# A decoder layer on one core: the opening with eight gate blocks per row block and half of x read turned, and four convolution blocks held behind points of VectorE's order

## The chip, the cores and the metric

The program runs on one core of one Trainium2 chip. The metric is the device time of one launch in microseconds (us). The profile comes from one further execution of the same program.

Names of the engines: TensorE (PE) multiplies matrices, with weight loads (PEld) beside them; VectorE (DVE), ScalarE (ACT) and GpSimd (POOL) work on tiles; SyncE (SP) only issues DMAs here. Each engine works through its own instructions in order, and waits on semaphores of the others.

## The reference

One layer of a hybrid decoder, D = 1024, 512 tokens, all in float32:

```
mod = silu(c) @ ada_w + ada_b;  sh1, sc1, g1, sh2, sc2, g2 = split(mod, 6)
u = rms_norm(x, mix_pre_g) * (1 + sc1) + sh1
qk_raw, v, o_pre, gates, glu = split(u @ w_in)
q, k = split(silu(causal_dwconv(qk_raw, 4 taps)))
h = mlstm_chunkwise(q, k, v, gates)          # 4 heads of 256, chunks of 128
h = rms_norm(h) * sigmoid(o_pre)
a, gt = split(glu)
y = silu(layer_norm(causal_dwconv(a * sigmoid(gt), 31 taps)))
mix = concat(h, y) @ w_out;  x = x + g1 * rms_norm(mix)
u = rms_norm(x, ffn_pre_g) * (1 + sc2) + sh2
a, gt = split(causal_dwconv(u @ ffn_up, 3 taps))
x = x + g2 * rms_norm((silu(gt) * a) @ ffn_down)
```

The change concerns `u`, the `glu` columns, the 31-tap convolution, and through the order of VectorE the heads.

## The kernel before

**Layout.** Channels lie on partitions, tokens along the free axis. D makes 8 row blocks of 128 channels (`KT`), the tokens 4 tiles of 128 (`NT`). x arrives with tokens on partitions and has to be turned.

**Products.** Each operand is split into a high part rounded to the fast matmul type and a low part, the rest; a product is three matmuls, high·high, high·low, low·high, summed in PSUM (`mm3`, L188 to L190). ScalarE rounds the high part of a weight, GpSimd subtracts for the low part (`w_split`, L170, L171).

**Order.** TensorE and SyncE run in the order in which the program is written. The order on VectorE, ScalarE and GpSimd is chosen at build time by a list scheduler with priorities (`tc.cur_priority += LATER` puts work behind), except in a stretch under `in_order()`, which keeps the written order. `tc.add_manual_dep(..., NoSync ...)` makes one instruction stand behind another on its engine without a semaphore.

**Opening (L225 to L340, in order).** For each token tile VectorE and ScalarE sum x², VectorE makes `xs`, GpSimd its power −1/2, VectorE scales the two halves of x (`x_scale`, L237), and TensorE turns 128x128 blocks (`turn_x`, L232), 32 in all; ScalarE copies them out of PSUM (`x_out`). Then for each row block k:

- SyncE loads `adaT[k]` (1 MB, 128 x 2048, pool `raws` of two buffers, `first_load`) one row block ahead, and `w_glu0[k]` (six gate blocks, 128 x 768, pool `adas` of two buffers, L306).
- VectorE sums the two halves of `adaT[k]` against silu(c), which lies broadcast in PSUM (`cps`; `junk`, L319); two small operations make scale and shift (`gsk`, L322, L323).
- ScalarE makes u's high part `uh` (L328) and u itself (L330); GpSimd makes the low part `ul` (L331; VectorE for k = 0) and the weights' low parts.
- TensorE adds the row block to six PSUM banks, 6 x 3 matmuls of 128x512 (L338; for k < 2 pass by pass over the banks, afterwards bank by bank with `mm3`).

The six banks are gate blocks 0 to 2, each with a half `a` and a half `gt`. Blocks 3 to 7 follow with whole projections (ten banks, weights loaded 1 MB each). `glu_gate` (L352, L354) makes the convolution's input `gt`.

**Convolution.** Each of 8 channel blocks has 31 taps: ScalarE does one, 25 run on VectorE over a PSUM bank `cv` (L661), 5 as a `side` sum on ScalarE and GpSimd (L655, L657); `ydl` (L671) then adds to the moments. The loop stands behind the heads' code at lower priority (`LATER`), so the scheduler puts taps where VectorE would be free. The two `cv` banks come from `cvpool`, which takes the place of `cspool` (the PSUM of `cps`) once that is closed.

**Heads.** Per head six projections (`head_proj`; q and k pass a 4-tap convolution, `conv4`, L414, last tap `d = 3`), `v`, the decay `Md` (L535) and `E` (L540, L542) from `Mb` (L533), scores `s` (L455) that VectorE multiplies into `E` (L456), output `o` (L466), its norm `hn` (L482), turned by TensorE (`hT`, L488), times the gate `so` (L490), and split (`hh` L493, `hl` L494). `s`, `o` and `hT` share two PSUM banks (`atbank`): a bank is free when its reader is through.

**Modulation.** `ada_block(i)` (L153 to L155) loads half of an `adaT` block from ScalarE's queue into the two `adas` buffers, and VectorE sums it against `cb`, silu(c) in SBUF. Blocks 16 to 23 stand behind the last convolution tap. Mixing and ConvFFN follow; the change doesn't touch them.

Of the kernel before, what the change touches and what calls it, by code (L numbers as in the profile page):

```python
# [10 lines left out]
F32 = mybir.dt.float32  # L11
# [6 lines left out]
P = 128  # L18
D = 1024
# [33 lines left out]
def decoder_layer(ctx, tc, w_glu0, x, c, adaT, vecs, w_glu, w_qko, w_v0, w_v, w_out, w_up, w_down, out):  # L53
# [175 lines left out]
    nc.sync.dma_start(vec[:, :FIRST], vecs[:, :FIRST])  # L229
# [4 lines left out]
    xT_ps = [mmbank(f"xT{j}") if j % 6 < 4 else atbank(f"xT{j}") for j in range(KT)]  # L234
    def x_scale(tt, xs):
        for hf in range(2):
            V.tensor_scalar(out=xn[tt][hf], in0=xn[tt][hf], scalar1=xs[:, 1:], scalar2=None, op0=ALU.mult)  # L237
            for i in range(NT if hf == 0 else 2):
                turn_x(NT * hf + i, tt)
# [3 lines left out]
    xss = []  # L243
    xjunks = [slot(f"xjunk{hf}") for hf in range(2)]
    for tt in range(NT):
        xsq = small.tile([P, 2], F32, tag="adap", name=f"xsq{tt}")
        for hf in range(2):
            xjunk = xjunks[hf]
            if hf:
                V.scalar_tensor_tensor(out=xjunk, in0=xn[tt][hf], scalar=1.0, in1=xn[tt][hf], op0=ALU.mult, op1=ALU.mult, accum_out=xsq[:, hf:])  # L250
            else:
                S.activation(xjunk, xn[tt][hf], AF.Square, accum_out=xsq[:, :1])
        if tt:
            x_scale(tt - 1, xss[tt - 1])
        if tt == 1:
            S.activation(cb, cps, AF.Silu)
        if tt == NT - 1:
            S.activation(cps, cps, AF.Silu)
        xs = small.tile([P, 2], F32, tag="gsk", name=f"xs{tt}")
        V.tensor_scalar(out=xs[:, :1], in0=xsq[:, :1], scalar1=xsq[:, 1:], scalar2=D * EPS, op0=ALU.add, op1=ALU.add)  # L260
        G.tensor_tensor(out=xs[:, 1:], in0=xs[:, :1], in1=mhalf[:, :1], op=ALU.pow)
        xss.append(xs)
    x_scale(NT - 1, xss[-1])
# [7 lines left out]
    for j in range(6, KT):  # L271
        for tt in range(NT):
            turn_x(j, tt)
# [21 lines left out]
    G0 = 6  # L295
# [6 lines left out]
    banks0 = [mmbank(f"glu{i}") if i < 4 else atbank(f"glu{i}") for i in range(G0)]  # L302
    for k in range(KT):
        wk = []
        r = adas.tile([P, D], F32, tag="ada", name=f"wglu0_{k}")
        nc.sync.dma_start(r[:, : G0 * P], w_glu0[k])  # L306
        if k == 0:
            for j in range(3):
                x_out(j, S)
        for a, n in ((0, T), (T, (G0 - 4) * P)):  # L310
            wk.append(w_split(r[:, a : a + n], f"wglu0_{k}_{a}"))
# [4 lines left out]
        part = small.tile([P, 2], F32, tag="adap", name=f"adap{k}")  # L316
        for i in range(2):
            junk = small.tile([P, D], BF16, tag="junk", bufs=1, name=f"junk{k}_{i}")
            V.scalar_tensor_tensor(out=junk, in0=first[k][:, i * D : (i + 1) * D], scalar=1.0, in1=cps, op0=ALU.mult, op1=ALU.mult,  # L319
                                   accum_out=part[:, i : i + 1])  # L320
        gsk = small.tile([P, 2], F32, tag="gsk", name=f"gsk{k}")
        V.tensor_scalar(out=gsk[:, :1], in0=part[:, :1], scalar1=bp1[:, k : k + 1], scalar2=g32[:, k : k + 1], op0=ALU.add, op1=ALU.mult)  # L322
        V.tensor_scalar(out=gsk[:, 1:], in0=part[:, 1:], scalar1=vcol("ada_b", 2 * k + 1), scalar2=None, op0=ALU.add)  # L323
        if k == 0:
            x_out(3, S)
            V.tensor_scalar(out=xr[0], in0=xr[0], scalar1=gsk[:, :1], scalar2=gsk[:, 1:], op0=ALU.mult, op1=ALU.add)
        hi, lo = u[k]
        S.activation(hi, xT_ps[0] if k == 0 else xr[k], AF.Identity, scale=gsk[:, :1], bias=gsk[:, 1:])  # L328
        if k:
            S.activation(xr[k], xr[k], AF.Identity, scale=gsk[:, :1], bias=gsk[:, 1:])  # L330
        (G if k else V).tensor_tensor(out=lo, in0=xr[k], in1=hi.bitcast(F32), op=ALU.subtract)  # L331
        if k == 0:
            for j in (6, 7, 4, 5):
                x_out(j, S)
        if k < 2:
            for a, b in ((0, 0), (1, 0), (0, 1)):
                for i, ps in enumerate(banks0):
                    PE.matmul(ps, blk(wk, i)[a], u[k][b], start=k == 0 and a == b, stop=False)  # L338
# [6 lines left out]
    cspool.__exit__(None, None, None)  # L345
    cvpool.append(ctx.enter_context(tc.tile_pool(name="cvpool", bufs=2, space=PSUM)))
# [61 lines left out]
    def conv4(ps, i, name):  # L408
# [4 lines left out]
        for d in range(1, 4):  # L413
            V.scalar_tensor_tensor(out=t[:, d:], in0=ps[:, : T - d], scalar=w(3 - d), in1=t[:, d:], op0=ALU.mult, op1=ALU.add)  # L414
# [7 lines left out]
    heads = {}  # L422

# [6 lines left out]
    def head_proj(h, i):  # L430
# [113 lines left out]
    for i in range(3):  # L544
        head_proj(0, i)
# [708 lines left out]
```

## Time and profile before

| what | us |
|---|---|
| three runs | 781.28, 781.31, 781.71 |
| median | 781.31 |
| profiled execution | 782.39 |
| its span (first to last instruction) | 780.6 |
| TensorE busy | 761.7 |
| VectorE busy | 591.3 |
| ScalarE busy | 407.6 |
| GpSimd busy | 383.9 |

Starts in the trace count from the start of the span. The profiled execution lies 1.08 over the median, and its span leaves out 1.8 around it. In a row of the timeline stand start, duration, engine, line, operation, out<-in, form, count, and in brackets how long the engine was idle before it and who ended that. Matmuls overlap: their pitch is less than their duration.

### The profile page before, as it was taken

The page shows a single profiled execution, that of the slowest core. Times are in us where ns is not written, and L with a number is a line of the kernel's source. Part 1 is how long each engine was busy: PE and PEld are TensorE (multiplying, and loading weights), DVE is VectorE, ACT ScalarE, POOL GpSimd, SP SyncE. Part 2 cuts the span into 40 slices and gives each one's busy share as a digit, 9 for nine tenths or more (in the row PEclk, how much of TensorE's full clock was granted, in tenths as well). Part 3 has the DMA queues.
Part 4 walks back from the last instruction along what each step waited for, and adds up shares of the span by engine and source line. Part 5 has one row for each costly group of instructions (what it writes and reads, how often), then busy time and mean ns, then how long its engine had stood idle before and what let it go on. Part 6 is the DMA issues. An engine that isn't in the chain of part 4 may idle for free.

```text
span 780.6 us, 10572 instructions
## 1 busy us (share of the span) xinstructions
PE 761.7 (98%) x3683; PEld 635.0 (81%) x3683; DVE 591.3 (76%) x938; ACT 407.6 (52%) x766; POOL 383.9 (49%) x313
## 2 busy tenths in 40 slices
PE   7899999999999999999999999999999999999996
PEld 4678898878888888888878998888888888888884
DVE  7659999999998533555868799665556677699997
ACT  6576428668655554482244445444444444456762
POOL 3689759779778534334661446544454440000001
PEclk9999999999999999999999999999999999999998
DMA  8973313303117432424952763332333321777862
GB/s 297 325 293 126 107 58 108 135 29 109 55 57 248 154 103 86 143 105 144 391 196 103 242 230 136 129 108 93 124 115 128 116 101 61 260 273 235 299 241 108
DMA packets 35977, 124.28 MB, mean 159 GB/s; under 512 B 4146, under 2 KB 5586, under 8 KB 29908
## 3 DMA queue, kind: packets, MB, share of 16 engines
q1 hardware_dynamic: 24084, 95.15, 34.8%
q10 hardware_dynamic: 11840, 28.46, 10.2%
q8 instruction: 29, 0.48, 0.2%
q14 instruction: 24, 0.20, 0.1%
HBM read 112.17 MB, written 11.42 MB: 158 GB/s over the span
## 4 chain that ended last, share of the span: by engine, by line
PE 80%; DVE 10%; DMA 4%; issue 3%; POOL 1%; ACT 1%; ACTq 0%; POOLq 0%; DVEq 0%; SPq 0%
PE up L189 10%; PE up L188 10%; PE up L190 10%; DVE cv L661 5%; PE qko L188 4%; PE qko L189 4%; PE qko L190 4%; PE p L190 4%; PE p L189 4%; PE p L188 4%; PE glu L189 3%; PE glu L190 3%; PE glu L188 3%; DMA spare<-in_adaT 2%; PE o L466 2%
## 5 line engine op out<-in xcount | busy, mean ns | idle before, releaser
L661 DVE SCALAR_TENSOR_TENSOR cv<-gt,cvw,cv 128x506 f32<-128x506 f32 (+24 forms) x200 | 134.2, 728 | 0.4
L617 POOL TENSOR_TENSOR ro2r<-ro2t,mhalf 128x1 f32<-128x1 f32 x1 | 0.5, 538 | 120.7 <-DVE ro2t L615 120.7
L171 POOL TENSOR_TENSOR wup_1024l<-wup,wup_1024h 128x512 fp32r<-128x512 f32 x20 | 27.8, 1388 | 31.6 <-ACT wup_1024h L170 22.2
L171 POOL TENSOR_TENSOR wup_0l<-wup,wup_0h 128x512 fp32r<-128x512 f32 x20 | 27.8, 1388 | 29.4 <-ACT wup_0h L170 29.4
L657 POOL TENSOR_TENSOR cs<-cs,cs 128x510 f32<-128x510 f32 (+3 forms) x32 | 42.0, 1312 | 0.2
L171 POOL TENSOR_TENSOR wup_1536l<-wup,wup_1536h 128x512 fp32r<-128x512 f32 x20 | 28.4, 1422 | 27.2 <-ACT wup_1536h L170 27.2
L189 PE MATMUL up<-u2l,wup_0h 128*128 128x512 f32 (+1 forms) x100 | 36.5, 365 | 0.2 <-DVE u2l L830 0.2
L188 PE MATMUL up<-u2h,wup_0h 128*128 128x512 f32 (+1 forms) x100 | 36.5, 365 | 0.0
L188 PE MATMUL up<-u2h,wup_1024h 128*128 128x512 f32 (+1 forms) x100 | 36.4, 364 | 0.0
L190 PE MATMUL up<-u2h,wup_0l 128*128 128x512 f32 (+1 forms) x100 | 36.4, 364 | 0.0
L188 PE MATMUL up<-u2h,wup_512h 128*128 128x512 f32 (+1 forms) x100 | 36.4, 364 | 0.0
L189 PE MATMUL up<-u2l,wup_512h 128*128 128x512 f32 (+1 forms) x100 | 36.4, 364 | 0.0
L190 PE MATMUL up<-u2h,wup_512l 128*128 128x512 f32 (+1 forms) x100 | 36.4, 364 | 0.0
L188 PE MATMUL up<-u2h,wup_1536h 128*128 128x512 f32 (+1 forms) x100 | 36.4, 364 | 0.0
L189 PE MATMUL up<-u2l,wup_1536h 128*128 128x512 f32 (+1 forms) x100 | 36.4, 364 | 0.0
L190 PE MATMUL up<-u2h,wup_1536l 128*128 128x512 f32 (+1 forms) x100 | 36.4, 364 | 0.0
L190 PE MATMUL up<-u2h,wup_1024l 128*128 128x512 f32 (+1 forms) x100 | 36.4, 364 | 0.0
L189 PE MATMUL up<-u2l,wup_1024h 128*128 128x512 f32 (+1 forms) x100 | 36.3, 363 | 0.0
L155 DVE SCALAR_TENSOR_TENSOR junk<-ada,cb 128x1024 bf16<-128x1024 f32 x20 | 31.0, 1551 | 7.0 <-DMA ada<-in_adaT 6.7
L171 POOL TENSOR_TENSOR wup_512l<-wup,wup_512h 128x512 fp32r<-128x512 f32 x20 | 27.2, 1358 | 14.6 <-ACT wup_512h L170 14.6
L655 ACT ACTIVATE cs<-gt,cvw 128x511 f32<-128x511 f32 (+4 forms) x40 | 27.2, 712 | 5.0 <-POOL cs L657 4.1
L171 POOL TENSOR_TENSOR wqko_1024l<-wqko,wqko_1024h 128x512 fp32r<-128x512 f32 x12 | 16.6, 1380 | 21.9 <-PE v L189 12.3
(1061 smaller groups left out, 2680.6 us busy)
## 6 DMA issues: line engine op xcount, KB each, us to landing
wup<-in_w_up SPq DMA_DIRECT2D x22, 1024.0 KB, 8.3
wqko<-in_w_qko SPq DMA_DIRECT2D x12, 1024.0 KB, 5.0
ada<-in_adaT ACTq DMA_DIRECT2D x20, 512.0 KB, 5.9
ada<-in_adaT SPq DMA_DIRECT2D x16, 512.0 KB, 5.9
wo<-in_w_out SPq DMA_DIRECT2D x8, 1024.0 KB, 9.2
spare<-in_adaT ACTq DMA_DIRECT2D x12, 512.0 KB, 7.3
wglu<-in_w_glu SPq DMA_DIRECT2D x5, 1024.0 KB, 7.7
wd<-in_w_down SPq DMA_DIRECT2D x6, 768.0 KB
```

What stands on the lines that cost most here:

```text
L155: t = V.scalar_tensor_tensor(out=junk, in0=r, scalar=1.0, in1=cb, op0=ALU.mult, op1=ALU.mult, accum_out=mod[:, i : i + 1])
L171: (eng or G).tensor_tensor(out=lo[:, :n], in0=src, in1=hi[:, :n].bitcast(F32), op=ALU.subtract)
L188: PE.matmul(ps, a[0], b[0], start=start, stop=False)
L189: PE.matmul(ps, a[0], b[1], start=False, stop=False)
L190: PE.matmul(ps, a[1], b[0], start=False, stop=stop)
L466: PE.matmul(o[:, : DH + 2], E[h][cc][:, a : a + P], vs[h][cc], start=cc == 0, stop=cc == tt)
L617: G.tensor_tensor(out=r, in0=t, in1=mhalf[:, :1], op=ALU.pow)
L655: S.activation(t[:, d:], cvx[j][:, : T - d], AF.Copy, scale=w(CK - 1 - d))
L657: G.tensor_tensor(out=side[:, d:], in0=side[:, d:], in1=t[:, d:], op=ALU.add)
L661: last_tap = V.scalar_tensor_tensor(out=cp[:, d:], in0=cvx[j][:, : T - d], scalar=w(CK - 1 - d), in1=cp[:, d:], op0=ALU.mult, op1=ALU.add)
```

## The change

**Opening.** It takes eight gate blocks (`G0 = 8`, `w_glu0[k]` 128 x 1024): gate blocks 0 to 3; banks 6 and 7 are the two of `cvpool`, which opens earlier. Blocks 4 to 7 follow with eight projections. Only row blocks 0 to 3 of x are turned on TensorE, by a matmul with a diagonal tile `dg` (the identity times the token's factor, on VectorE, 128x128), which turns and scales at once; the same diagonal with `ones` gives the factors along the free axis (`rb`). Row blocks 4 to 7 come turned from memory (`xT`, 0.26 MB each, issued by SyncE in k = 1 to 4) and are scaled by VectorE (L348 of the new kernel). The sums run one row block ahead (`ada_sum(k + 1)`, around `ul`) and read `cb` in SBUF; all low parts are made on VectorE.

**Convolution.** The loop's body becomes `cv_block(j, behind)`. Blocks 0 to 3 are as before; the first tap of block 4 stands behind the last conv4 tap of head 0, of blocks 5, 6 and 7 behind those of projections (1, 0), (1, 3) and (2, 1).

```diff
-    def turn_x(j, tt):
-        PE.transpose(xT_ps[j][:, tt * P : (tt + 1) * P], xn[tt][j // NT][:, j % NT * P : (j % NT + 1) * P], ident)
...
-    def x_scale(tt, xs):
-        for hf in range(2):
-            V.tensor_scalar(out=xn[tt][hf], in0=xn[tt][hf], scalar1=xs[:, 1:], scalar2=None, op0=ALU.mult)
...
+    def x_turn(tt, xs):
+        dg = slot(f"dg{tt}")[:, :P]
+        V.tensor_scalar(out=dg, in0=ident, scalar1=xs[:, 1:], scalar2=None, op0=ALU.mult)
+        for j in range(TURNED):
+            PE.matmul(xT_ps[j][:, tt * P : (tt + 1) * P], xn[tt][j // NT][:, j % NT * P : (j % NT + 1) * P], dg, start=True, stop=True)
+        PE.matmul(rb_ps[:, tt * P : (tt + 1) * P], ones, dg, start=True, stop=True)
...
+    def ada_sum(k, i):
...
+        V.scalar_tensor_tensor(out=junk, in0=first[k][:, i * D : (i + 1) * D], scalar=1.0, in1=cb, op0=ALU.mult, op1=ALU.mult,
+                               accum_out=part[k][:, i : i + 1])
...
-    G0 = 6
+    G0 = 8
...
         if k == 1:
             nc.sync.dma_start(vec[:, FIRST:], vecs[:, FIRST:])
+        if 1 <= k <= TURNED:
+            j = TURNED + k - 1
+            nc.sync.dma_start(xr[j], xT[j - TURNED])
...
+        if k >= TURNED:
+            V.scalar_tensor_tensor(out=xr[k], in0=xr[k], scalar=gs, in1=rb, op0=ALU.mult, op1=ALU.mult)
+        for b in range(2):
+            wk[b] = w_split(r[:, b * T : (b + 1) * T], f"wglu0_{k}_{b}", eng=V)
...
+        if k + 1 < KT:
+            ada_sum(k + 1, 0)
+        if k < TURNED:
+            V.tensor_tensor(out=lo, in0=xr[k], in1=hi.bitcast(F32), op=ALU.subtract)
+        else:
+            V.scalar_tensor_tensor(out=lo, in0=xr[k], scalar=sh, in1=hi.bitcast(F32), op0=ALU.add, op1=ALU.subtract)
+        if k + 1 < KT:
+            ada_sum(k + 1, 1)
+        if k < 4:
+            passes(wk, k, range(G0))
         else:
...
+    CV_BEHIND = {(1, 0): 5, (1, 3): 6, (2, 1): 7}
...
+        if (h, i) in CV_BEHIND:
+            cv_block(CV_BEHIND[h, i], last_conv4[0])
...
+    head0_tap = last_conv4[0]
...
+            if behind is not None:
+                tc.add_manual_dep(last_tap[0].ins, behind.ins.name, mybir.DependencyInfo(mybir.DependencyClass.NoSync, mybir.DependencyReason.DATA),
+                                  reason="order on VectorE")
+                behind = None
...
+    for j in range(5):
+        cv_block(j, head0_tap if j == 4 else None)
```

VectorE in the opening, from the shift of one row block to that of the next but one; before:

```order
L323 TENSOR_SCALAR gsk_433<-adap_428,vec 128x1
L319 SCALAR_TENSOR_TENSOR junk_0_471,adap_470<-ada_425,cps 128x1024
L319 SCALAR_TENSOR_TENSOR junk_1_473,adap_470<-ada_425,cps 128x1024
L322 TENSOR_SCALAR gsk_475<-adap_470,bp_210,g_212 128x1
L323 TENSOR_SCALAR gsk_475<-adap_470,vec 128x1
```

and now, at row block 4 (`xr_221` its x, `rb_s` the factors, `wglu_4` its weights, `adap` the sums):

```order
L331 TENSOR_SCALAR gsk_440<-adap_404,bp_213,g_215 128x1
L332 TENSOR_SCALAR gsk_440<-adap_404,vec 128x1
L348 SCALAR_TENSOR_TENSOR xr_221<-xr_221,gsk_440,rb_s 128x512
L171 TENSOR_TENSOR wglu_4_0l<-wglu_4_434,wglu_4_0h 128x512
L171 TENSOR_TENSOR wglu_4_1l<-wglu_4_434,wglu_4_1h 128x512
L271 SCALAR_TENSOR_TENSOR junk_0_454,adap_453<-ada_436,cb 128x1024
L361 SCALAR_TENSOR_TENSOR ul<-xr_221,gsk_440,uh 128x512
L271 SCALAR_TENSOR_TENSOR junk_1_457,adap_453<-ada_436,cb 128x1024
L331 TENSOR_SCALAR gsk_488<-adap_453,bp_213,g_215 128x1
```

VectorE's four operations per row block have become eight, and the sums stand one row block ahead of their scale and shift.

VectorE ahead of head 0's `hn` (`cv_1699`, `cv_1748` and, in the new kernel, `cv_1702`, `cv_1877` are two blocks' sums of taps; the tap's number is 512 less the width); before, rows 303 to 309:

```order
L661 SCALAR_TENSOR_TENSOR cv_1699<-gt_874,cvw,cv_1699 128x491
L661 SCALAR_TENSOR_TENSOR cv_1748<-gt_945,cvw,cv_1748 128x499
L661 SCALAR_TENSOR_TENSOR cv_1699<-gt_874,cvw,cv_1699 128x490
L661 SCALAR_TENSOR_TENSOR cv_1748<-gt_945,cvw,cv_1748 128x498
L661 SCALAR_TENSOR_TENSOR cv_1699<-gt_874,cvw,cv_1699 128x489
L482 TENSOR_SCALAR hn_0_1962<-hn_0_1962,fac_2052 128x256 x2
L482 TENSOR_SCALAR hn_1_1963<-hn_1_1963,fac_2052 128x256 x2
```

and now, rows 302 to 308:

```order
L694 SCALAR_TENSOR_TENSOR cv_1702<-gt_770,cvw,cv_1702 128x488
L694 SCALAR_TENSOR_TENSOR cv_1877<-gt_841,cvw,cv_1877 128x499
L694 SCALAR_TENSOR_TENSOR cv_1702<-gt_770,cvw,cv_1702 128x487
L694 SCALAR_TENSOR_TENSOR cv_1877<-gt_841,cvw,cv_1877 128x498
L694 SCALAR_TENSOR_TENSOR cv_1702<-gt_770,cvw,cv_1702 128x486
L512 TENSOR_SCALAR hn_0_1831<-hn_0_1831,fac_1970 128x256 x2
L512 TENSOR_SCALAR hn_1_1832<-hn_1_1832,fac_1970 128x256 x2
```

Before, these are the last two blocks of eight; now they are the sixth and the seventh, one is left for later, and 155 taps stand ahead of `hn` instead of 177.

VectorE behind head 1's output (`hn`, then `so` and `hl`) up to head 2's first `E`; before, from the first of `hn`:

```order
L482 TENSOR_SCALAR hn_0_2413<-hn_0_2413,fac_2503 128x256 x2
L482 TENSOR_SCALAR hn_1_2414<-hn_1_2414,fac_2503 128x256 x2
L155 SCALAR_TENSOR_TENSOR junk_3199,mod<-ada_3197,cb 128x1024
L160 TENSOR_TENSOR mod<-mod,vec 128x8
L599 SCALAR_TENSOR_TENSOR gains<-mod,vec 128x8
L535 TENSOR_TENSOR Md_2541<-Mb_2539,cmask 128x512
L490 SCALAR_TENSOR_TENSOR so_4_2041<-so_4_2041,hT_0_2654 128x512
L490 SCALAR_TENSOR_TENSOR so_5_2086<-so_5_2086,hT_1_2664 128x512
L494 SCALAR_TENSOR_TENSOR hl_0_2661<-so_4_2041,ghalf,hh_0_2660 128x512
L494 SCALAR_TENSOR_TENSOR hl_1_2671<-so_5_2086,ghalf,hh_1_2670 128x512
L456 SCALAR_TENSOR_TENSOR E_2543<-s_0_2753,E_2543 128x512
```

and now, from block 7's last tap (`cv_2298`), which follows `Md`:

```order
L694 SCALAR_TENSOR_TENSOR cv_2298<-gt_912,cvw,cv_2298 128x482
L155 SCALAR_TENSOR_TENSOR junk_3138,mod<-ada_3136,cb 128x1024
L155 SCALAR_TENSOR_TENSOR junk_3142,mod<-ada_3140,cb 128x1024
L708 SCALAR_TENSOR_TENSOR ydl_2342<-ysum,gt_912 128x512
L155 SCALAR_TENSOR_TENSOR junk_3146,mod<-ada_3144,cb 128x1024
L520 SCALAR_TENSOR_TENSOR so_4_1959<-so_4_1959,hT_0_2621 128x512
L155 SCALAR_TENSOR_TENSOR junk_3150,mod<-ada_3148,cb 128x1024
L520 SCALAR_TENSOR_TENSOR so_5_2004<-so_5_2004,hT_1_2631 128x512
L524 SCALAR_TENSOR_TENSOR hl_0_2628<-so_4_1959,ghalf,hh_0_2627 128x512
L155 SCALAR_TENSOR_TENSOR junk_3154,mod<-ada_3152,cb 128x1024
L524 SCALAR_TENSOR_TENSOR hl_1_2638<-so_5_2004,ghalf,hh_1_2637 128x512
L155 SCALAR_TENSOR_TENSOR junk_3158,mod<-ada_3156,cb 128x1024
```

The last tap, which stood ahead of these sums well before head 1's output, now stands behind it, and the eight sums stand between it and head 2's `E`. Seven of the eight stood ahead of `hn` before.

More of the change, by code (lines that the diff above doesn't have):

```diff
@@ L245, in decoder_layer @@
+    xT_ps = [mmbank(f"xT{j}") for j in range(TURNED)]
+    rb_ps = atbank("rb")
+    last = None
     for tt in range(NT):
         xsq = small.tile([P, 2], F32, tag="adap", name=f"xsq{tt}")
[L247 to L252, printed above, removed]
@@ L265, in decoder_layer @@
+    for i in range(2):
+        ada_sum(0, i)
     bp1 = const.tile([P, KT], F32, name="bp1")
@@ L324, in decoder_layer @@
+        hi, lo = u[k]
         if k == 0:
[L325 to L331, printed above, removed]
```

103 lines of the change are left out of this document (55 added, 48 removed).

## The prediction

> **What bounds the kernel now.** First the page: how long each engine is busy.
>
> ```profile
> span 780.6 us, 10572 instructions
> PE 761.7 (98%) x3683; PEld 635.0 (81%) x3683; DVE 591.3 (76%) x938; ACT 407.6 (52%) x766; POOL 383.9 (49%) x313
> ```
>
> TensorE works for 98% of the span, so an edit gains only where it removes one of TensorE's waits, or starts its stream earlier. Next the list of TensorE's waits: who ended them, total, times, longest.
>
> ```profile
> PE glu L189 <- POOL ul L331: 2.4, 3, 1.3
> ...
> PE hT L488 <- DVE hn L482: 1.4, 1, 1.4
> PE gT L585 <- DVE gains L783: 1.2, 1, 1.2
> PE glu L338 <- ACT uh L328: 1.1, 1, 1.1
> PE hT L488 <- ACT E L542: 0.4, 1, 0.4
> ```
>
> The waits with `glu` are the opening's; `hT` is a head's output being turned; `gT` lies far behind the change. Third, TensorE's own rows: the opening's first gate matmul, two waits in it, its pitch (ten steps from the first to the second of the 28.66 and 30.92 rows: 0.227 us each), and the first matmul behind it.
>
> ```profile
> 16.99 1.47 PE L338 MATMUL glu<-uh,wglu_0h 128*128 128x512 f32 x4 [1.07 <-ACT uh L328]
> 27.39 0.50 PE L189 MATMUL glu<-ul,wglu_0h 128*128 128x512 f32 x1 [0.87 <-POOL ul L331]
> 28.66 0.39 PE L188 MATMUL glu<-uh,wglu_0h 128*128 128x512 f32 x1
> ...
> 30.92 0.39 PE L189 MATMUL glu<-ul,wglu_512h 128*128 128x512 f32 x1
> ...
> 33.07 0.50 PE L189 MATMUL glu<-ul,wglu_0h 128*128 128x512 f32 x1 [1.31 <-POOL ul L331]
> ...
> 54.22 0.39 PE L188 MATMUL glu<-uh,wglu_0h 128*128 128x512 f32 x1
> ```
>
> The opening has 144 matmuls (8 row blocks, 6 banks, 3 products), 32.7 us at 0.227. It takes 54.22 − 16.99 = 37.2, so 4.5 us of it are lost to waiting: a row block's operands are not ready when its matmuls could start. A window over this stretch, with a later one for comparison:
>
> ```profile
> core 0: us, PE busy (x) PEld busy (x) DVE busy (x) ACT busy (x) POOL busy (x), PEclk, DMA share, GB/s
> 17.00:54.20 37.20, 34.80 (x144) 26.66 (x145) 21.79 (x48) 23.06 (x39) 27.47 (x26) 1.00 0.92 325
> 680.00:690.00 10.00, 10.00 (x46) 8.29 (x45) 10.00 (x18) 5.24 (x11) 0.00 (x0) 1.00 0.85 306
> ```
>
> The granted clock is full, the DMA engines are 92% busy at 325 GB/s: loads are what the opening waits for.
>
> ```profile
> L319 DVE SCALAR_TENSOR_TENSOR junk<-ada,cps x16: 1209/1220/1222, 13.3 to 45.2; 128x1024 bf16<-128x1024 f32 x16
>   DMA ada<-in_adaT: 8.6, 7
> ```
>
> VectorE's sums wait 8.6 us in all for the modulation weights. Per row block the opening moves 1.05 + 0.39 MB, 4.44 us at 325 GB/s, for 18 × 0.227 = 4.09 us of matmuls. It asks for more bytes than its matmuls have time for.
>
> **The change, term one: the start.** VectorE's rows that lead to the first gate matmul, and ScalarE's:
>
> ```profile
> 11.46 0.21 DVE L260 TENSOR_SCALAR xs<-xsq 128x1 f32<-128x1 f32 x1
> 12.34 0.88 DVE L237 TENSOR_SCALAR xn<-xn,xs 128x512 f32<-128x512 f32 x2 [0.67 <-POOL xs L261]
> 13.28 1.21 DVE L319 SCALAR_TENSOR_TENSOR junk<-ada,cps 128x1024 bf16<-128x1024 f32 x1
> ...
> 15.69 0.27 DVE L322 TENSOR_SCALAR gsk<-adap,bp,g 128x1 f32<-128x1 f32 x1
> 16.14 0.80 ACT L328 ACTIVATE uh<-xT,gsk 128x512 fp32r<-128x512 f32 x1
> ```
>
> Two 128x512 scalings (0.88) per token tile become one of 128x128, taken as 0.2 by the small rows. `xs` of the last tile stands behind the scaling of the tile before, 0.8 of pitch that becomes 0.2: it comes near 10.9 instead of 11.46; its factor is there 0.88 later as now; the scaling ends near 11.9 and the sums start near 12.0, 1.28 earlier. Two small operations (L266, L269) move behind the sums: 0.15 back. First gate matmul near 15.9: **−1.1**. The matmuls with the diagonal stand where transposes stood; their price in fp32 isn't in the trace; four fewer blocks are turned.
>
> **Term two: eight banks.** 192 matmuls stand in the opening; before, the same 192 end 48 × 0.227 = 10.9 behind 54.22, at 65.1, because TensorE runs there without a gap. With no wait at all they would now end at 15.9 + 43.6 = 59.5: −5.6 at most, the start's part in it. The bytes are 1.57 MB per row block plus 0.26 in each of k = 1 to 4, against 24 × 0.227 = 5.45 us: 4.84 us at 325 GB/s without x, 5.65 with it. From 17 us some 10.75 MB are left (mine, from the tile sizes and what had landed), 33 us, until 50: not the bound on the whole, close to it in the four blocks with x.
>
> VectorE takes over the splits and `ul`. Their price is not uniform:
>
> ```profile
> 17.21 1.04 DVE L331 TENSOR_TENSOR ul<-xr,uh 128x512 fp32r<-128x512 f32 x1
> 51.38 1.30 POOL L171 TENSOR_TENSOR wglu_512l<-wglu,wglu_512h 128x512 fp32r<-128x512 f32 x1
> 697.13 0.68 DVE L927 TENSOR_TENSOR t_5l<-wd,t_5h 128x512 fp32r<-128x512 f32 x1
> 697.73 0.68 DVE L1014 TENSOR_TENSOR wdmore<-wdmore 128x512 f32<-128x512 f32 x1
> L155 DVE SCALAR_TENSOR_TENSOR junk<-ada,cb x20: 1208/1428/2236, 233.3 to 470.4; 128x1024 bf16<-128x1024 f32 x20
> ```
>
> A difference of two tiles in SBUF takes 1.04 beside a working GpSimd (17.21) and a pitch of 0.60 with GpSimd idle (the 680 window: GpSimd 0.00). GpSimd has nothing queued between the factors and block 4's splits, so I take 0.60. Per block on VectorE: two sums 2 × 1.26 with their read-out, the two scalars 0.4, two splits 1.2, `ul` 0.6: 4.7; from k = 4 on also the scaling of x, 0.65: 5.35. TensorE has 5.45. So VectorE fits, by 0.7 and then by 0.1. I price four places where it doesn't: at k = 1, `cvw`, which reads the second part of the vectors and ran at 22.20 so far (row below, where that load was through), now stands between the scale and the shift of the row block: if that load lands at 20.5 (it is no later than 22.2, its issue before 17), `cvw`, a small one, the shift and `uh` (0.29, 0.17, 0.2, 0.8) are through at 22.0, and TensorE is there at 15.9 + 5.45 = 21.3: 0.75; at k = 4, the first scaling of x ahead of `ul`: 0.3; at k = 7, GpSimd starts on block 4's splits and slows `ul`: 0.4; 0.15 at the start. Together 1.6 (0 to 3.7).
>
> ```profile
> 22.20 0.29 DVE L373 TENSOR_SCALAR cvw<-vec 128x248 f32<-128x248 f32 x1
> ```
>
> Opening's end 59.5 + 1.6 = 61.1, against 65.1: **−4.0**, call it −4.1 (bounds −2.0 and −5.6).
>
> [...]
>
> **Term three: the hold on the taps.** Around the first head's output:
>
> ```profile
> 206.89 0.28 PE L190 MATMUL v<-wv_5h,ul 128*128 128x256 f32 x1
> 208.53 0.30 PE L488 MATMUL hT<-ident,hn 128*128 128x128 f32 x1 [1.36 <-DVE hn L482]
> 203.57 4.56 DVE L661 SCALAR_TENSOR_TENSOR cv<-gt,cvw,cv 128x492 f32<-128x492 f32 x7
> 208.04 1.13 DVE L482 TENSOR_SCALAR hn<-hn,fac 128x256 f32<-128x256 f32 x4
> ```
>
> TensorE would turn `hn` at 207.0 and gets it at 208.53; VectorE is in taps (0.64 each) without a gap until 208.04. In the order of before 177 taps stand ahead of this `hn`, in the new one 155: 22 × 0.64 = 14.1 less, and two gates and one `ydl` less, 2.0. Against that, taps start later: before they began when gates 0 and 1 were in, near 54.4; now their banks serve gates 6 and 7, free behind the opening and four gates, near 64: +9.6. VectorE reaches `hn` near 208.0 − 16.1 + 9.6 = 201.5. TensorE wants it at 207.0 − 4.1 = 202.9. The wait goes: **−1.6** with its restart (0 to −1.8).
>
> **Term four: what the hold leads to.** The taps now end behind head 1's output, so the eight sums of modulation blocks 16 to 23 stand where they were long done before: ahead of `so` (which frees the bank of the next scores `s`) and of `E`. Rows of the same place before:
>
> ```profile
> 254.20 0.40 PE L533 MATMUL Mb<-Ms,rowsel 128*128 128x512 f32 x1
> 259.39 0.68 DVE L535 TENSOR_TENSOR Md<-Mb,cmask 128x512 f32<-128x512 f32 x1
> 264.15 0.93 ACT L404 ACTIVATE v<-v 128x256 f32<-128x256 f32 x3
> 267.39 1.02 PE L455 MATMUL s<-q_0c,k_2c 128*128 128x512 f32 x2
> DMA to landing us min/median/max: 4.8/6.3/10.2
> ```
>
> Two of these loads sit in the two buffers; the third is issued on ScalarE only behind `E` (4.8 us behind `Md`), and only when a sum has freed a buffer. With 5.7 gained ahead, `Mb` is there at 254.2 + 0.2 − 5.7 = 248.7, `Md` runs near 249.0 behind it, since no sum stands ahead of it any more, and the third load goes out near 253.8. It lands 4.8 to 6.3 later (the row above, of those loads), at 258.6 to 260.1; its sum 1.25 and `so` 0.65 end at 260.5 to 262.0. TensorE wants the bank at 267.39 − 5.7 − 0.5 = 261.2 (0.5: the wait on `E` of the list, which goes since `E` comes no later than now). The same again for the second `so`, whose load has its own buffer: in all 0 to 3.4, I take 1.7, the middle. Net **+1.2**. Later, the orders of both kernels are the same on every engine, and I carry nothing on.
>
> **Sum.** −4.1 − 1.6 + 1.2 = −4.5. The profiled execution took 782.39 (span 780.6 and 1.8 around it), 1.1 more than the median of the runs, 781.31; the difference goes onto the median: **776.8**.
>
> **Rivals.**
> 1. *Nothing new waits*: VectorE hides all, loads land by 5 us. −5.6 − 1.6 + 0.5 of wait gone: 781.31 − 6.7 = 774.6. For it: VectorE's sum fits. Against: it fits by 0.1 us.
> 2. *The loads pace the opening.* Before, 16 sums in 8 row blocks start from 13.3 to 45.2: (45.2 − 13.3 − 1.3) / 7 = 4.4 per block, at 1.44 MB. At 1.57 and 1.83 MB that is 4.8 and 5.6; and `ul`, now between the two sums, holds each of the two buffers 0.6 longer, 0.3 a block: 5.1 and 5.9, against 5.45. The four blocks with x lose 0.45 each, 1.8 in all, on top of the 1.6: opening's gain 2.2, time 781.3 − 2.2 − 1.6 + 1.2 = 778.7. For it: seven waits on loads before, and 92% busy DMA engines. Against: loads are issued more than a block ahead of their use.
> 3. *Slower: the modulation loads behind the heads.* They take the row's largest, 10.2 us, since weights of the next head load at once. Each of the two `so` and then `E` is late by about 4 more: stalls 8, sum −4.1 − 1.6 + 8 − 0.5 = +1.8: 783. It decides from loads over about 9 us; the median 6.3 speaks against.
> 4. *Slower: VectorE contended in the opening*, at 1.04 per difference and 1.43 and more per sum: 6.3 to 7.2 per block instead of 5.35, some 8 × 1.2 lost, opening +3.8: 784.7. It decides once GpSimd reads beside more than a third of it; it has nothing queued.
> 5. *The hold doesn't hold*: then `hn` waits as now and term four falls: 781.3 − 4.1 = 777.2. The order shows that it does hold; the number lies within the forecast's range.
>
> **How the numbers follow.** Forecast with rival 5: 0.55; rival 1: 0.14; rival 2: 0.19, half of it within no change; rival 3: 0.08; rival 4: 0.04. 0.2%, 1.6 us, is about what a measurement of this kernel can tell from no change. Faster 0.55 + 0.14 + 0.09 = 0.78, same 0.10, slower 0.12. The range leaves out the slower cases and little else: 774.2 to 780.8.
>
> **What would show it.** First gate matmul near 15.9; 192 gate matmuls ending near 61; waits on `ul` of under 2 us, at k = 1, 4 and 7; VectorE's differences at 0.6; no wait of `hT` on `hn` at head 0; a wait of `s` on `so` of 1 to 3 us near 261. Wrong would be sums over 1.3 in the opening, sums waiting on `ada` for over 3 us there, or a wait that stands further behind, where I carried nothing on.

## The result and the profile after

| | before | after |
|---|---|---|
| runs (us) | 781.28 to 782.37, four | 774.21 to 777.37, four |
| median | 781.51 | 775.43 |
| profiled execution | 782.39 | 775.40 |
| its span | 780.6 | 773.7 |
| first gate matmul | 16.99 | 15.56 |
| first matmul behind the same 192 gate matmuls | 65.10 | 60.92 |

The ratio of the new time to the old is 0.992, with a 95% interval from 0.9907 to 0.9932, clear of 1: 0.8% faster, by 6.1 us in the medians where 4.5 were forecast, and inside the range of 774.2 to 780.8. The page of the changed kernel, its first lines:

```profile
span 773.7 us, 10579 instructions
PE 757.7 (98%) x3691; PEld 635.8 (82%) x3691; DVE 605.3 (78%) x961; ACT 400.6 (52%) x753; POOL 351.8 (45%) x286
```

TensorE is still busy for 98%. Of the 6.9 us by which the span shrank, 2.9 are idle time of TensorE by the two pages and 4.0 were counted as busy, so its waits show only a part of the gain; its starts, further below, show the whole. The list of its waits (who ended them, total, times, longest):

```profile
PE glu L316 <- ACT uh L336: 2.0, 1, 2.0
PE glu L316 <- ACT uh L352: 1.4, 1, 1.4
...
PE s L485 <- DVE E L486: 0.6, 1, 0.6
PE aT L589 <- DVE ga L584: 0.4, 1, 0.4
```

Of the waits of before, those on `ul` in the opening (2.4), on `hn` (1.4), on `gains` (1.2) and on head 2's `E` (0.4) are gone. New are one on `uh` at row block 1, one of `s` on `E`, one of `aT`; the one on `uh` ahead of the first gate matmul has grown from 1.1 to 2.0. The first row behind 192 gate matmuls in the kernel before:

```profile
65.10 0.39 PE L188 MATMUL glu<-uh,wglu_0h 128*128 128x512 f32 x1
```

and TensorE's rows in the opening now, with the same row at their end:

```profile
15.56 1.20 PE L316 MATMUL glu<-uh,wglu_1h 128*128 128x512 f32 x4 [2.01 <-ACT uh L336]
...
22.71 0.50 PE L316 MATMUL glu<-uh,wglu_0h 128*128 128x512 f32 x1 [1.41 <-ACT uh L352]
...
60.92 0.39 PE L188 MATMUL glu<-uh,wglu_0h 128*128 128x512 f32 x1
```

From 15.56 the 192 matmuls would need 43.6 us, until 59.1; they end at 60.9, so 1.8 are lost, nearly all at 22.71. The window over the opening (columns as before):

```profile
15.50:54.00 38.50, 37.03 (x162) 30.35 (x163) 36.66 (x72) 19.16 (x33) 1.63 (x2) 1.00 0.96 349
```

VectorE works 36.7 of 38.5 us, the DMA engines are 96% busy, and TensorE yet waits once. Why it waits there, VectorE's rows say:

```profile
21.27 0.29 DVE L398 TENSOR_SCALAR cvw<-vec 128x248 f32<-128x248 f32 x1 [0.98 <-DMA vec<-in_vecs]
21.47 0.17 DVE L444 TENSOR_SCALAR ghalf<-vec 128x8 f32<-128x8 f32 x1
21.54 0.21 DVE L332 TENSOR_SCALAR gsk<-adap,vec 128x1 f32<-128x1 f32 x1
```

The shift of row block 1 (L332) stands behind `cvw`, which waits for the second part of the vectors, and `uh` needs the shift.

At head 0, VectorE's normalisation `hn` and TensorE's turning of it, which no longer waits:

```profile
201.81 1.13 DVE L512 TENSOR_SCALAR hn<-hn,fac 128x256 f32<-128x256 f32 x4
203.05 1.04 PE L518 MATMUL hT<-ident,hn 128*128 128x128 f32 x8
```

Where the 7.1 us between the two profiles arise, from TensorE's starts of the same instruction in both (after minus before, as it grows): −1.43 at the first gate matmul; −4.18 behind the opening; −3.74 at `aT`, where TensorE now waits for VectorE behind taps; −5.48 at head 0's `hT`, whose wait on `hn` is gone; −6.50 behind head 1's `hT`; −5.79 at head 2's third `s`, which waits for `E`; −7.11 at `gT`, whose wait on `gains` is gone. Behind that nothing changes by more than 0.1.

### The profile page after: what moved, and what is told of

Read it like the earlier page. It is cut to its first block, busy times and chain, and to the rows that moved or that the text cites. A ratio compares the mean times of both kernels' runs of the same rounds, so it can differ in the third digit from the quotient of the medians.

```text
span 773.7 us, 10579 instructions
## 1 busy us (share of the span) xinstructions
PE 757.7 (98%) x3691; PEld 635.8 (82%) x3691; DVE 605.3 (78%) x961; ACT 400.6 (52%) x753; POOL 351.8 (45%) x286
## 3 DMA queue, kind: packets, MB, share of 16 engines
q10 hardware_dynamic: 11984, 28.48, 10.6%
## 4 chain that ended last, share of the span: by engine, by line
PE 75%; DVE 18%; DMA 3%; ACT 2%; issue 1%; POOL 0%; SPq 0%; POOLq 0%; DVEq 0%; ACTq 0%
PE up L190 10%; PE up L189 10%; PE up L188 10%; DVE cv L694 10%; PE p L190 4%; PE p L188 4%; PE p L189 4%; PE glu L190 3%; PE glu L189 3%; PE glu L188 3%; PE glu L316 2%; PE mixa L190 2%; PE mixa L188 2%; PE mixa L189 2%; PE mixb L189 2%; PE mixb L188 2%
## 5 line engine op out<-in xcount | busy, mean ns | idle before, releaser
L694 DVE SCALAR_TENSOR_TENSOR cv<-gt,cvw,cv 128x489 f32<-128x489 f32 (+23 forms) x200 | 136.8, 727 | 3.1 <-ACT cv L682 2.1
L171 POOL TENSOR_TENSOR wup_1536l<-wup,wup_1536h 128x512 fp32r<-128x512 f32 x20 | 28.1, 1403 | 27.5 <-ACT wup_1536h L170 27.5
L170 ACT ACTIVATE wup_1024h<-wup 128x512 fp32r<-128x512 f32 x22 | 13.9, 631 | 24.7 <-PE up L189 20.1
```

The costliest lines, as they stand in the source:

```text
L170: S.activation(hi[:, :n], src, AF.Copy)
L171: (eng or G).tensor_tensor(out=lo[:, :n], in0=src, in1=hi[:, :n].bitcast(F32), op=ALU.subtract)
L694: last_tap[0] = V.scalar_tensor_tensor(out=cp[:, d:], in0=cvx[j][:, : T - d], scalar=w(CK - 1 - d), in1=cp[:, d:], op0=ALU.mult, op1=ALU.add)
```

## The experiments

Each kernel differs from one of the two as its diff shows. Each is compared with runs of the kernel before on the same chip; the ratio is its time over theirs, with a 95% interval in brackets.

**The new opening alone.** The convolution as before, without the hold.

```diff
-    CV_BEHIND = {(1, 0): 5, (1, 3): 6, (2, 1): 7}
+    CV_BEHIND = {}
...
-    for j in range(5):
-        cv_block(j, head0_tap if j == 4 else None)
+    for j in range(KT):
+        cv_block(j)
```

> The new opening alone: all eight convolution blocks stand in one loop behind the heads' code as before, none is held behind a point of VectorE. My theory on record gives the opening -4.2 us (first gate matmul at 15.6, one wait of 1.6 us at row block 1) and the hold the -1.9 at head 0's hn and the cost at head 2. By that, this kernel takes 777.3 and TensorE still waits 1.5 us or more for hn at head 0. The rival: the wait on hn goes because the taps start 9 us later and the scheduler itself then puts fewer of them ahead of hn (146 stand there in this kernel's order, 155 with the hold, 177 before); then it is gone here too. By the rival head 1 pays instead, since a sum whose load is not in flight yet now stands ahead of head 1's hn: 775.5 plus 0 to 3 us there.

782.29 (12 runs), against 781.85 of before beside it: ratio 1.0001 (0.9979 to 1.0022). **Without the hold the whole gain is gone**, more than either theory allowed. TensorE's waits:

```profile
PE s L485 <- DVE so L520: 2.0, 1, 2.0
...
PE hT L518 <- DVE hn L512: 1.4, 1, 1.4
PE s L485 <- DVE E L486: 1.3, 2, 1.0
```

The opening gains its 4.2 as in the full change, and the wait on `hn` at head 0 is gone here too, as the rival said (the `hn` row above is head 1's). Then VectorE is late at three places in a row. The first, VectorE and TensorE behind head 0's `hn`:

```profile
201.18 0.68 DVE L565 TENSOR_TENSOR Md<-Mb,cmask 128x512 f32<-128x512 f32 x1
201.78 7.11 DVE L694 SCALAR_TENSOR_TENSOR cv<-gt,cvw,cv 128x503 f32<-128x503 f32 x11
208.80 1.27 DVE L520 SCALAR_TENSOR_TENSOR so<-so,hT 128x512 f32<-128x512 f32 x2
...
209.53 0.70 PE L485 MATMUL s<-q_0c,k_2c 128*128 128x512 f32 x1 [1.98 <-DVE so L520]
```

Eleven taps that the scheduler put ahead of `so` keep the bank of `s` occupied. At head 1 it is a sum: its load went out behind 253.26, from ScalarE, and landed at 256.8. `hn` stands behind this sum on VectorE, and then waits for GpSimd's factors `fac`, which took 2.01 beside the sum (1.03 in the changed kernel):

```profile
253.26 2.57 ACTq L153 DMA_DIRECT2D ada<-in_adaT  x2
...
256.84 2.25 DVE L155 SCALAR_TENSOR_TENSOR junk<-ada,cb 128x1024 bf16<-128x1024 f32 x1 [0.78 <-DMA ada<-in_adaT]
...
257.96 2.01 POOL L509 TENSOR_TENSOR fac<-ssq,mhalf 128x4 f32<-128x4 f32 x1
...
260.01 2.13 DVE L512 TENSOR_SCALAR hn<-hn,fac 128x256 f32<-128x256 f32 x4 [0.92 <-POOL fac L509]
```

**The hold alone**, on the opening of before: `cv_block` with its `behind`, and `CV_BEHIND`, put into the kernel before.

```diff
-    for j in range(KT):
...
+    def cv_block(j, behind=None):
...
+        tc.cur_priority += LATER
         cp = cvbank(f"cv{j}")
...
+    for j in range(5):
+        cv_block(j, head0_tap if j == 4 else None)
```

> The hold alone, on the opening of before. 153 taps stand ahead of head 0's hn instead of 177, and the taps still start at 54.4. If the hold is what removes the wait on hn, that wait is gone: -1.9. The sums of modulation blocks 16 to 23 stand behind head 1's output as in the changed kernel, so a wait of s on E of 0.7 should stand at head 2, and the wait on E before it (0.5) be gone. 781.5 - 1.9 + 0.2 = 779.8. The rival, that without the later start of the taps the hold moves nothing that TensorE waits for, gives 781.5.

780.25 (12 runs), ratio 0.9969 (0.995 to 0.9989): −1.6. The wait on `hn` at head 0 is gone, and `s` waits on `E` as forecast (0.5 where 0.7 was expected). Behind the opening this wait is left, besides one of 0.2 on `u2l`:

```profile
PE s L460 <- DVE E L461: 0.5, 1, 0.5
```

So each part alone removes the wait on `hn`: in both orders fewer taps stand ahead of it (146 with the opening alone, 153 with the hold alone, 177 before). And the two parts do not add up: opening alone 0, hold alone −1.6, together −6.1.

**The wait at row block 1 taken away.**

```diff
+            vec_behind = V.scalar_tensor_tensor(out=lo, in0=xr[k], scalar=sh, in1=hi.bitcast(F32), op0=ALU.add, op1=ALU.subtract)
...
+    late = V.tensor_scalar(out=cvw, in0=vcols("cv_dw_w", 0, CK * KT), scalar1=0.5, scalar2=None, op0=ALU.mult)
+    tc.add_manual_dep(late.ins, vec_behind.ins.name, mybir.DependencyInfo(mybir.DependencyClass.NoSync, mybir.DependencyReason.DATA),
+                      reason="order on VectorE")
...
```

The copy `ghalf`, which reads the same vectors, gets the same dependency.

> The changed kernel with the copies cvw and ghalf, which read the second part of the vectors, put behind the low part of u of row block 7 on VectorE, so that VectorE no longer waits for that load between the scale and the shift of row block 1. Nothing else moves. If this wait is the whole loss in the new opening, TensorE's 1.57 us there go, the opening runs without a gap from its first matmul, and the time falls by 1.5 to 773.9. The rival: the next thing is late then (a load of modulation weights, a split), and less than 0.5 us is gained.

774.79 (6 runs, 773.95 to 776.34), ratio 0.9893 (0.986 to 0.9927); the changed kernel beside it 775.26. In the profile the wait is gone and no other stands in its place in the opening; from the first gate matmul to head 0's `v` TensorE takes 1.34 less than in the changed kernel's first profile, and 0.77 less than in its second (next run), where the same wait is 0.8 long instead of 1.4. Of that 0.5 shows in the medians, between what theory and rival forecast. The mechanism is shown; the size in the time is not separated from the spread of the runs.

**The changed kernel once more.** No edit.

> The changed kernel once more, beside the others on one chip. Its four runs so far spread from 774.2 to 777.4, more than those of before (781.3 to 782.4). If the 1.4 us that went at the row of gains is a collision of VectorE's sums with GpSimd's splits that falls out differently from one execution to the next, this profile shows other durations of these sums (between 1.2 and 2.3 us each) and may show the wait again; if it is a lasting part of the change, the wait is absent again.

775.26 (5 runs, 775.13 to 775.68). `gT` does not wait here either. The first gate matmul stands at 15.90 in this profile, and the row behind the 192 at 60.68: the opening's places move by a few tenths from one execution to the next.

**Six banks instead of eight, all else as changed.**

```diff
-    G0 = 8
+    G0 = 6
...
-        nc.sync.dma_start(r, w_glu0[k])
+        nc.sync.dma_start(r[:, : G0 * P], w_glu0[k][:, : G0 * P])
```

> The changed kernel with six gate blocks per row block in the opening instead of eight (blocks 3 to 7 follow as whole projections); x half turned, sums one block ahead, splits on VectorE and the hold stay. A row block has 18 x 0.227 = 4.09 us of matmuls then, VectorE works 4.4 on it for k < 4 and 5.1 from k = 4 on (durations of the changed kernel's profile), and the wait for the second part of the vectors at k = 1 is 1.4 longer since TensorE arrives earlier. My theory, that eight banks give TensorE enough work to cover what VectorE and the loads need: the opening loses about 7 us to waits instead of 1.6, the time is 780 to 781. The rival, that the earlier start and the new shares of the work alone bring the opening's gain and the number of banks is free: 775 to 776.5.

782.2 (11 runs), ratio 1.0004 (0.9988 to 1.0019): the gain is gone, as the theory said, and the time lies 1.2 over the 780 to 781 that it gave. TensorE's waits and the window of this kernel:

```profile
PE glu L189 <- DVE ul L361: 2.2, 2, 1.5
PE glu L316 <- ACT uh L336: 1.9, 1, 1.9
PE glu L188 <- ACT uh L355: 1.3, 2, 0.9
```

```profile
15.50:54.00 38.50, 34.58 (x131) 26.41 (x132) 35.12 (x72) 17.90 (x32) 2.88 (x2) 0.91 0.94 334
```

VectorE is nearly as busy (35.1 of 38.5) as with eight banks, and feeds 131 recorded matmuls instead of 162. Nearly the same VectorE work per row block is hidden by 24 matmuls and not by 18. The row behind the opening's 144 matmuls stands 2.8 later than in the kernel before. In this profile the granted clock of 0.91 has its share in that (two stretches of 3.4 us at 0.50, more on them below), but the result doesn't hang on it: TensorE waits for `uh` and `ul` again behind the second stretch, at 51.7 and 53.0, and the run at the median, 782.2, had a granted clock of 0.998 over its whole span.

**The splits back on GpSimd.**

```diff
-            wk[b] = w_split(r[:, b * T : (b + 1) * T], f"wglu0_{k}_{b}", eng=V)
+            wk[b] = w_split(r[:, b * T : (b + 1) * T], f"wglu0_{k}_{b}")
```

> The changed kernel with the low parts of the opening's weights made on GpSimd again for row blocks 1 to 7; VectorE has two instructions of 0.6 less per row block. The theory that VectorE keeps its pace only because GpSimd is idle: the sums, with two inputs in SBUF, go from 1.22 to between 1.4 and 2.2 us and ul from 0.6 to about 1, and VectorE's work per row block is 4.6 to 6 us instead of 4.7 and 5.35; the opening's end moves back by 1 to 3 us, the time to 776.5 to 778.5. The rival: since VectorE has 1.2 us less to do per row block, the slower sums fit, and the opening ends within 0.4 us of the changed kernel's, 775.3.

780.74 (11 runs), ratio 0.9984 (0.9974 to 0.9994): 2.2 over the forecast's upper end. The sums in the changed kernel, then in this one:

```profile
L271 DVE SCALAR_TENSOR_TENSOR junk<-ada,cb x16: 1215/1218/1226, 11.5 to 48.8; 128x1024 bf16<-128x1024 f32 x16
```

```profile
L271 DVE SCALAR_TENSOR_TENSOR junk<-ada,cb x16: 1209/1986/2314, 11.6 to 53.2; 128x1024 bf16<-128x1024 f32 x16
```

Beside GpSimd's subtractions a sum takes 1.99 in the median instead of 1.22 (from 15.5 to 54, GpSimd is busy for 23.0 us here and for 1.6 in the changed kernel). VectorE has 14 instructions less to do and is behind all the same: its last sum of the opening starts at 53.2 instead of 48.8, it is busy for 37.8 of the 38.5 us from 15.5 to 54, and the first matmul behind the opening stands at 64.5 instead of 60.9. (In this profile TensorE also lost 1.8 at a granted clock of 0.50, between 25.1 and 28.6. But at 48.3 it waits for VectorE's `ul` again and has no gap behind that, so at full clock it would have waited there the longer.) The wait on head 0's `hn` is back: the first tap stands at 69.9 instead of 64.9, 157 stand ahead of `hn`, and VectorE reaches it at 207.7 instead of 201.8. The forecast had priced the opening alone (1 to 3 us; it ends 3.6 later) and not this wait.

**Two waits taken away**: the edit of the row block 1 run, and four of the eight sums behind head 2's second `E`.

```diff
-        ada_block(i, last_tap[0])
+        ada_block(i, last_tap[0] if i < 20 else e_op[2, 1])
```

> The changed kernel with two waits taken away: cvw and ghalf behind row block 7's ul (no wait at row block 1), and four of the eight sums of modulation blocks 16 to 23 behind head 2's second E (no sum with a late load ahead of the first E). If each wait goes without another in its place: 1.1 us off at the opening's end as in the run with the first edit alone, and 0.7 at head 2 (s on E): 773.6. The rival: at head 2 the four sums stand ahead of the third E instead, and the wait moves there: 774.6.

773.64 (4 runs, 773.06 to 774.19), ratio 0.9893 (0.988 to 0.9907), and 774.65 and 773.62 on two other chips. In the profile the waits are gone, and TensorE is 2.4 us ahead of the changed kernel behind head 2. What stands in its list besides the first microseconds:

```profile
PE glu L316 <- ACT uh L336: 1.9, 1, 1.9
PE xT L242 <- DVE dg L240: 1.2, 1, 1.2
PE up L189 <- DVE u2l L875: 0.2, 1, 0.2
```

This version beats the kernel before on each of three chips. Over the changed kernel it is 0.6 to 1.8 better by the medians, with intervals that meet, and never beside it on one chip: that it is the faster of the two is not shown.

**The kernel before, once more**, for the wait on `gains`.

> The kernel before once more, with a profile. In its first profile gT waits 1.4 us for the row of gains; there VectorE's copy of 128x8 took 1.33 us and ran beside a GpSimd split, while in five profiles of other variants it took 0.16 and gT did not wait. If this is a collision that falls out differently from one execution to the next, the wait is likely absent here and the span about 1.2 shorter than 780.6; if it is a lasting trait of the kernel before, the wait and the 1.33 stand here again.

The span is 781.7, so no shorter: the opening and a wait of `hT` on `E` (1.5) lost more this time. But `gT` does not wait. VectorE's copy in the first profile of before, in this one, and in the changed kernel:

```profile
398.01 1.33 DVE L784 COPY gains<-mod 128x8 f32<-128x8 f32 x1
```

```profile
400.14 0.16 DVE L784 COPY gains<-mod 128x8 f32<-128x8 f32 x1
```

```profile
391.42 0.16 DVE L824 COPY gains<-mod 128x8 f32<-128x8 f32 x1
```

The scaling behind this copy, which is the last step to `gT`, took 1.32, 0.17 and 1.22. So the 1.4 us that the first two profiles differ by at `gT` are no lasting part of the change: they stood in one of two executions of the kernel before, which was also 0.9 over its median, and in none of the twelve profiles of other kernels does `gT` wait more than 0.2. How many of the runs before have this wait is not known.

**More bytes in the opening.**

```diff
             nc.sync.dma_start(xr[j], xT[j - TURNED])
+            nc.sync.dma_start(dram.tile([P, T], F32, tag=f"extra{k}", name=f"extra{k}"), xT[j - TURNED])
```

> The changed kernel with 0.26 MB more to move in each of row blocks 1 to 4: behind the load of x's turned block SyncE issues a copy of the same block from memory to memory, which nobody reads. Between 15.5 and 54 us the changed kernel's DMA engines are 93 to 102% busy at 312 to 388 GB/s, and TensorE waits once. If the loads have a block's slack, as rows that wait nowhere for a load after row block 1 suggest, the time stays within 0.5 us of the changed kernel's 775.3. The rival of my prediction, that the loads pace the opening or stand just at the point where they would: 1.05 MB at 350 GB/s are 3.0 us, and TensorE waits for them; 776.5 to 778.5.

The copies go from memory to memory, behind the loads of x in k = 1 to 4. 776.31 (6 runs, 775.5 to 779.28), 0.9 and 1.05 over the changed kernel's two medians, which are from other chips: between the two answers. In the profile the opening is not longer:

```profile
15.50:54.00 38.50, 37.23 (x161) 30.18 (x162) 36.60 (x73) 18.96 (x32) 0.96 (x1) 1.00 1.00 377
```

The DMA engines went from 96 to 100% busy and from 349 to 377 GB/s, and the matmul behind the 192 stands at 61.03 instead of 60.92. So the loads had room for 1.05 MB more. How much more they had isn't shown. The profile has one wait that the changed kernel's has not, 0.4 of `hT` on `hn` at head 0, and lacks the 0.4 of `aT`; the 0.9 of the runs is not explained by it.

**Work for TensorE in its first wait**, on the version with two waits taken away, and that version again beside it and once before.

```diff
+    for _ in range(3):
+        PE.matmul(banks0[7], ident, cb[:, :T], start=True, stop=True)
```

> The version with two waits taken away (cvw and ghalf behind row block 7, four of the eight sums behind head 2's second E), once more beside the other run on one chip: 773.6 again, within 0.5, and again no wait of s on E and no wait at row block 1.

> The version with two waits taken away, and three matmuls of 128x512 between the last turning of x and the first gate matmul, into a bank that the gate matmuls start anew afterwards: work that nobody reads. In one of its two profiles the granted clock fell to 0.50 between 17 and 20 us, behind 2.3 us in which TensorE had nothing to do; there 1.2 us were lost that no wait shows, and its runs beside that profile were 774.4 to 775.3 against 773.1 to 774.2. If that idle time is what takes the clock down, it stays at 1.00 here and the time is 773.6, also where the same kernel without the matmuls has 774.6. The rival: the three matmuls come late, delay the first gate matmul, and the time is 774.6 or more.

> The version with two waits taken away, beside the run with the three extra matmuls, on the same chip. By its two earlier runs 773.6 (clock 1.00 behind the first gate matmul) or 774.6 (clock 0.50 there for some 3 us).

In this order: 774.65 (4 runs, out of the forecast's 773.6 by more than 0.5), 774.02 (5 runs, 772.65 to 775.9, extra matmuls) and 773.62 (5 runs). In the first of these profiles the granted clock (the last column but two) fell behind a wait of 2.3; in the one with the extra matmuls the wait is gone and the clock did not fall:

```profile
13.00:15.40 2.40, 0.22 (x2) 0.03 (x1) 2.17 (x7) 1.89 (x4) 0.00 (x0) 1.00 1.02 416
15.40:17.00 1.60, 1.52 (x6) 1.28 (x7) 1.50 (x3) 1.60 (x5) 0.00 (x0) 0.94 1.05 420
17.00:20.00 3.00, 3.00 (x8) 2.33 (x8) 2.97 (x6) 1.56 (x3) 0.00 (x0) 0.50 1.01 399
```

```profile
15.50:18.00 2.50, 2.50 (x12) 1.88 (x11) 2.46 (x4) 2.35 (x6) 0.00 (x0) 1.00 1.04 405
18.00:20.00 2.00, 2.00 (x11) 1.65 (x10) 1.97 (x6) 0.52 (x1) 0.00 (x0) 1.00 1.01 401
```

The third profile, without extra matmuls, kept 1.00 as well, and the medians of 774.02 and 773.62 do not separate. Whether the filled wait is worth anything in the time stays open.

## Why the prediction was right, and where it was not

**The start**, −1.1 forecast, −1.43 measured (−1.09 in the changed kernel's second profile): scalings of 128x128 follow each other after 0.2 as assumed, and the sums start at 11.52 instead of the 12.0 forecast.

**The opening**, −4.1 forecast (its own terms give −4.0), −4.18 measured, by a slightly different account. That the numbers agree so closely is in part luck. The four stalls of 1.6 in all became one of 1.6: the one at row block 1, named with its cause, was sized at 0.75 because the load of the vectors was taken to land at 20.5; it landed just ahead of `cvw`, which ran at 21.27. Those at k = 4 and k = 7 did not appear. VectorE's sum of 5.35 against TensorE's 5.45 held: 36.7 of 38.5 us busy, differences 0.60 apart (their rows say 0.68 each), sums at 1.22. The experiment with six banks shows that the eight are what covers this work, the one with GpSimd that VectorE's rate beside an idle GpSimd (1.22 a sum, 1.99 with GpSimd at work) is a condition of it. The rival of loads that pace the opening fell: 1.05 MB more did not lengthen it in the profile. The step that said "loads are what the opening waits for", from DMA engines 92% busy at 325 GB/s, took 325 for what they can move. The changed kernel's opening moved 349 GB/s and the one with more bytes 377, so 325 was no limit; what bounded the opening of before was not tested.

**The hold** came out in its sum and failed as an explanation. The sum: 155 taps, the first at 64.9 (64 forecast), `hn` at 201.8 (201.5 forecast), and −1.6 forecast where TensorE's steps at `hT` and behind it are −1.5 and −0.4. The explanation: the step said that the wait on `hn` goes because 22 taps fewer stand ahead of it, by the hold. The opening alone takes that wait away too, since in its order only 146 stand ahead; that this comes from the later start of the taps is likely, but no run separates it. What the hold does is something that the prediction did not see: without it the late taps come ahead of `so` at head 0, and the sums ahead of `hn` and `E` at heads 1 and 2, and TensorE loses 2.1, 1.6 and 1.8 us there (with the hold, 0.8 remain of the last). The prediction had counted taps ahead of one instruction. The question was what stands ahead of every instruction of a head that TensorE waits for. Of the 6.1 us, the hold alone brings 1.6 and the opening alone nothing: the other 4.5 need both.

**Head 2**, +1.2 forecast: the place was right, the size and the waiting instruction were not. These are the rows of ScalarE's issue, the third sum, `so`, the last sum ahead of `E`, `E` and TensorE in the changed kernel:

```profile
253.79 0.33 ACTq L153 DMA_DIRECT2D ada<-in_adaT  x1
...
257.61 1.74 DVE L155 SCALAR_TENSOR_TENSOR junk<-ada,cb 128x1024 bf16<-128x1024 f32 x1 [0.71 <-DMA ada<-in_adaT]
259.28 0.68 DVE L520 SCALAR_TENSOR_TENSOR so<-so,hT 128x512 f32<-128x512 f32 x1
...
267.12 2.31 DVE L155 SCALAR_TENSOR_TENSOR junk<-ada,cb 128x1024 bf16<-128x1024 f32 x1
...
269.36 1.14 DVE L486 SCALAR_TENSOR_TENSOR E<-s,E 128x512 f32<-128x512 f32 x2
...
270.10 0.70 PE L485 MATMUL s<-q_0c,k_2c 128*128 128x256 f32 x2 [0.56 <-DVE E L486]
```

The third load went out at 253.79 (253.8 forecast), but landed 3.8 later, under the 4.8 taken as the least: `so` was through at 259.9, in time for 261. The sums behind it ran at 2.3 beside GpSimd instead of 1.25, and made `E` late: TensorE loses 0.8 there. With the wait on `E` before it gone (−0.6), head 2 costs 0.2, not 1.2. In the trace six of the eight sums stand ahead of the first `E`, not all eight, and the other two behind it. Leaving only four ahead took that wait away as well.

**Nothing carried on** was right for the runs, and wrong for this pair of profiles: the `gT` wait of before was one execution's. The prediction quoted it as a wait far behind the change and took it to stay. The wait of `aT` on `ga` behind taps (0.4) was not forecast.

The sum by places that were forecast, opening −4.2, head 0 −2.0, head 2 +0.2, with `aT` +0.4 and a small −0.2, is −5.7 in the two profiles, by their unrounded starts; the runs say −6.1.

**The other rivals.** That nothing new waits (rival 1) was priced at 774.6 with a slip of sign: the 0.5 of wait that goes is a gain, so its terms give −7.7 and 773.6. The measured 775.43 lies between the forecast and 774.6, and nearer to 774.6; it is the wait of 1.4 at row block 1 and the one at `E` that decide against this rival, not the number. The version with these two waits taken away took 773.64. Slow modulation loads (rival 3) and a contended VectorE in the opening (rival 4) did not occur: the third load took 3.8, and the opening's sums 1215 to 1226 ns. The wait on `hn` that rival 5 kept is gone.

## What to carry to other kernels

Two parts of a change that share an engine cannot be priced one by one: the opening made the first tap start 10.6 us later on VectorE (64.9 instead of 54.4), and only with the hold did the saved time survive the next consumers of that engine. When work is pushed back on an in-order engine, list every instruction behind it that the bounding engine waits for, and not only the one that waited before. A wait that appears in one profile is not yet a trait of the kernel; a second profile of the same kernel is the cheapest test.

## What the runs showed of the hardware

A sum of VectorE over 128x1024 that reads two tiles of SBUF took 1.22 us with GpSimd idle (the changed kernel's opening) and up to 2.31 beside GpSimd's subtractions (splits on GpSimd); subtractions of 128x512 on GpSimd took from 1.3 to 2.3 (1287 to 2282 ns in the changed kernel). The sums in the opening of before, which read one tile of SBUF and `cps` in PSUM, took 1209 to 1222 ns while GpSimd was busy for 27.5 of 37.2 us. A copy of 128x8 took 0.16 or 1.33, in the same place of the program: 1.33 where it ran beside a GpSimd subtraction (398.02 to 399.30 in the first profile of before), 0.16 in the changed kernel at 391.42, where one subtraction ends and the next begins (391.43). `cvw`, which like this copy reads one tile of SBUF, took 0.29 in the changed kernel, with GpSimd idle, and 1.16 beside GpSimd's subtractions (at 21.75, splits on GpSimd).

TensorE's granted clock fell to 0.50 four times behind the start of the gate matmuls, in three profiles (two waits taken away once more, splits on GpSimd, and twice with six banks). Each time it stayed there for about 3.4 us, worked out from the mean clock of windows (0.83 over the 10 us from 24 with splits on GpSimd, and over the 10 us from 34 with six banks), and the wait ahead of it was 2.3, 2.1, 1.9 and 1.5 us, in the order of the profiles named. In seven other profiles it stayed at 1.00 behind a wait of 1.9 to 2.0 at the first gate matmul. So the length of the wait alone does not separate the cases; what does is not shown, and only the extra matmuls, in one profile, tested whether the wait is the cause.

The price was 1.3 us in one profile, which no wait on the list shows: from the first gate matmul to the row behind the 192 it took 45.3, and 44.0 and 44.1 in the two other profiles of the same kernel. Between 17 and 20 us that profile has 8 recorded matmuls, at 0.50, and the first of the same kernel 15, at 1.00.
